# Modulation products of a two-layer diffusion step in groups of two blocks, their rows through GpSimd's queue

## The chip, the cores and the metric

One Trainium2 chip, one core. The metric is the device time of one execution in microseconds, as the median of three runs. The engines are TensorE (PE in the profile, its weight loads PEld), VectorE (DVE), ScalarE (ACT), GpSimd (POOL) and SyncE (SP), which only issues DMAs here. Each runs its own program in order and waits on semaphores of the others; DMAs issued from one engine stand in that engine's program too.

## The reference

Two layers over 128 context tokens and 512 latent tokens (640 columns), model width 1024. Every layer has six modulation vectors of 1024, for two conditioning vectors (context and latent):

```python
def _adaln(cond, w, b):
    return jax.nn.silu(cond) @ w + b

def _layer(x, mod, lw, lam_init, rope, ctx):
    sh1, sc1, g1, sh2, sc2, g2 = jnp.split(mod, 6, axis=-1)
    h = _rmsnorm(x, lw['norm1_g']) * (1.0 + sc1) + sh1
    mix, ctx_out = _mixers(h, lw, lam_init, rope, ctx)
    x = x + g1 * mix
    h = _rmsnorm(x, lw['norm2_g']) * (1.0 + sc2) + sh2
    x = x + g2 * _swiglu(h, lw['w_ffn_in'], lw['w_ffn_out'])
    return x, ctx_out
```

`_mixers` projects h to the inputs of retention, differential attention and latent attention (with compressed keys and values), merges the three branches by sigmoid gates and projects the result. The change concerns `silu(cond) @ w_ada`, a 1024 x 6144 matrix in each layer; in blocks of 128 columns that is 48 blocks a layer.

## The kernel before

Everything is float32, and the large matmuls are made of three products of rounded halves (names ending in hi and lo, `mm3`, line 134). A weight piece is loaded into one of three "raw" buffers by SyncE (`load_w`, line 126), ScalarE casts it to whi (line 118), VectorE forms wlo (line 121), and only then is the raw buffer free; whi and wlo have four buffers each.

The modulation is computed in three ways. In the beginning TensorE computes the first 16 blocks of layer 0. VectorE computes the blocks 16 to 39 of either layer in the retention's merge (`ada_rows`, its rows through GpSimd's queue into three "rawr" tiles). The others, blocks 40 to 47 of both layers and 0 to 15 of layer 1, are `ada_products`: 8 groups of four blocks. A group (l, j) loads four pieces of 512 KB, w_adap[l, j, i], by SyncE into the shared "raw" buffers (name rawp, line 265). Piece i holds the k-tiles 2i and 2i + 1, 512 columns each. The condition vector is stationary, 32 columns wide, two of them real; k-tile k goes to partition group k modulo 4 of one PSUM bank, G (line 269), so that four products can stand side by side in the array. ScalarE copies the bank to ada_r (line 272), four small matmuls with a selection matrix add up the partition groups and turn the result (line 276), VectorE adds the bias (line 279).

Where these groups stand is given by `plan` and `fill`: a list of steps from several generators, spread evenly over the fill points of a stage. In the latent attention (`mla`) the 30 steps of `diff_proj` (one projection of 128 tokens by 256 columns each, 24 matmuls, copied by ScalarE to stg, stored by GpSimd to the DRAM tile dproj, line 831) are mixed with 4 groups in layer 0 and 2 in layer 1, two steps a group. In the differential attention (`diff`) the gates (tile gt) and the values of the retention (tile gt, name rvs) are mixed with 2 groups in layer 0 and none in layer 1. While it fills, all of these take the same PSUM bank G. The tile framework then orders each engine's instructions by its own estimate of their times; it is the order that TensorE, SyncE and GpSimd follow.

Stages, in order, of each layer: mla, with w_mla, w_qp, w_qk, w_v as weights and normalised columns cqn turned and split (line 576, cqh, cql); the first branch (matmuls on yhi); diff, in which GpSimd loads V, rk, rq from dproj; retention (stores nret); merge with the other gates and branches, in which csr and rawr are loaded; output projection; FFN.

Of the kernel before, what the change touches and what calls it, by code (L numbers as in the profile page):

```python
# [12 lines left out]
F32 = mybir.dt.float32  # L13
# [8 lines left out]
P = 128  # L22
# [29 lines left out]
class Kern:  # L52
# [206 lines left out]
    def ada_products(self, pool, chunks):  # L259

        for l, j in chunks:
            ps = self.G()
            for i in range(4):
                raw = self.w.tile([P, 2, 512], F32, tag="raw", name="rawp", bufs=3)
                self.nc.sync.dma_start(out=raw, in_=self.io["w_adap"][l, j, i])
                for kk in range(2):
                    k = 2 * i + kk
                    g = k % 4
                    self.pe.matmul(ps[32 * g:32 * g + 32, :], self.cs[:, k, :], raw[:, kk, :],  # L269
                                   start=k < 4, stop=k >= 4, tile_position=(0, 32 * g))  # L270
            r = pool.tile([P, 512], F32, tag="ada_r", name="ada_r", bufs=1)
            self.act.copy(r, ps)
            yield 1
            ps = self.Tp()
            for c in range(4):
                self.pe.matmul(ps[:, 2 * c:2 * c + 2], r[:, 128 * c:128 * c + 128],
                               self.ct[:, C_SEL:C_SEL + 2], start=True, stop=True)
            b = self.pv[:, V_ADA + 48 * l + 4 * j:V_ADA + 48 * l + 4 * j + 4]
            self.dve.tensor_tensor(self.mod_tile(l)[:, 4 * j:4 * j + 4, :], ps[:, 0:8].rearrange("p (a v) -> p a v", v=2),
                                   b.unsqueeze(2).to_broadcast([P, 4, 2]), op=ALU.add)  # L280
            yield 1
# [1084 lines left out]
    def run(self):  # L1366
# [3 lines left out]
        for l in range(DEPTH):  # L1370
# [12 lines left out]
            with ExitStack() as c2:  # L1383
                pool = self.sb("mla", 1, c2)
                chunks = ((0, 10), (0, 11), (1, 0), (1, 1)) if l == 0 else ((1, 10), (1, 11))
                self.plan(37, (self.diff_proj(l, act, pool), 30, 0.0, 1.0), (self.ada_products(pool, chunks), 2 * len(chunks), 0.0, 1.0))
# [10 lines left out]
            chunks = ((1, 2), (1, 3)) if l == 0 else ()  # L1397
            self.plan(23, (self.gates(l, 2, act, m, mp), 16, 0.0, 0.7), (self.ret_values(l, act, mp), 20, 0.6, 0.95),
                      (self.ada_products(mp, chunks), 2 * len(chunks), 0.0, 0.7))
# [119 lines left out]
def layout(inputs):  # L1519
# [23 lines left out]
    out["w_adap"] = c(np.stack([[pieces(g["w_ada"][l][:, 512 * j:512 * j + 512], 2) for j in range(12)] for l in L]).reshape(DEPTH, 12, 4, 128, 2, 512))  # L1543
# [54 lines left out]
```

## Time and profile before

| | us |
|---|---|
| median of 3 runs | 2518.74 (2518.12 to 2518.92) |
| profiled execution | 2521.4 |
| its span, first to last instruction | 2519.6 |
| TensorE busy | 2415.9 (96%) |
| VectorE busy | 1769.7 (70%) |
| ScalarE busy | 1102.4 (44%) |
| GpSimd busy | 139.1 (6%) |
| mean granted clock of TensorE | 0.989 |

All later times come from the profiled execution. Busy is the time in which at least one instruction of the engine runs; matmuls overlap, so that a busy TensorE may still run at less than its full rate. The granted clock is a share of TensorE's upper level; 1.00 is 2.4 GHz, 0.50 is 1.2 GHz.

### The profile page before, as it was taken

To read this page: it belongs to the slowest core of one execution; us is meant where nothing else is said; L and a number is where in the kernel's file an instruction comes from. 1 tells how busy PE (TensorE), PEld (TensorE's weight loads), DVE (VectorE), ACT (ScalarE), POOL (GpSimd) and SP (SyncE) were. 2 spreads that over 40 slices of the span, in tenths; PEclk is the share of its full clock that TensorE was granted. 3 is DMA by queue.
4 is the path that set the end of the run, shared out by engine and by line. 5 is a ranking of instruction groups with operands and counts; after the bars stand their busy time and mean duration, and the time that the engine had idled before them with its cause. 6 is when DMAs were issued, how large, how long until landed. Compare 5 with 4: busy or idle time off the path is not lost.

```text
span 2519.6 us, 43242 instructions
## 1 busy us (share of the span) xinstructions
PE 2415.9 (96%) x16996; PEld 2330.6 (93%) x16996; DVE 1769.7 (70%) x3883; ACT 1102.4 (44%) x2265; POOL 139.1 (6%) x235
## 2 busy tenths in 40 slices
PE   8999999999999999999998999999999999999997
PEld 5899888999999999999987989989998999999997
DVE  5767677556688777767775766865666887777775
ACT  5555555522223633333374654655322354333334
POOL 0000211000010000000000002100000000000001
PEclk9999999999999999999999999999999999999999
DMA  6232423232454122222232122213215532222222
GB/s 265 78 102 86 133 99 104 79 114 68 151 176 133 53 92 75 89 77 73 78 123 83 60 94 88 89 55 110 84 65 197 166 93 74 86 76 82 76 73 72
DMA packets 81578, 250.02 MB, mean 99 GB/s; under 512 B 10624, under 2 KB 20064, under 8 KB 80352
## 3 DMA queue, kind: packets, MB, share of 16 engines
q1 hardware_dynamic: 58464, 180.91, 22.1%
q0 software_dynamic: 16864, 60.39, 7.3%
q10 hardware_dynamic: 6048, 5.98, 0.7%
q8 instruction: 133, 2.18, 0.4%
q14 instruction: 69, 0.57, 0.1%
HBM read 227.01 MB, written 20.22 MB: 98 GB/s over the span
## 4 chain that ended last, share of the span: by engine, by line
PE 81%; DVE 9%; ACT 3%; issue 3%; DMA 3%; POOL 0%; DVEq 0%; ACTq 0%; SPq 0%; POOLq 0%
PE G L134 33%; PE S L134 26%; PE Tp L134 7%; PE O L894 1%; PE S L1144 1%; PE S L1143 1%; PE S L1142 1%; PE Tp L697 1%; DVE wlo L121 1%; DVE x L1104 1%; ACT whi L118 1%; DMA rawp<-w_adap 1%; DVE v L1241 1%; PE G L269 1%; PE O L672 1%
## 5 line engine op out<-in xcount | busy, mean ns | idle before, releaser
L118 ACT CAST whi<-raw 128x1024 fp32r<-128x1024 f32 (+4 forms) x346 | 295.9, 858 | 463.8 <-PE S L134 174.2
L121 DVE TENSOR_TENSOR wlo<-raw,whi 128x1024 fp32r<-128x1024 f32 (+4 forms) x346 | 340.1, 985 | 138.6 <-ACT whi L118 136.8
L134 PE MATMUL G<-whi,hhi 128*128 128x256 f32 x1040 | 300.4, 289 | 8.0 <-DVE rvs L847 4.4
L134 PE MATMUL G<-whi,hlo 128*128 128x256 f32 x1040 | 295.9, 285 | 0.0
L134 PE MATMUL G<-wlo,hhi 128*128 128x256 f32 x1040 | 295.7, 284 | 0.0
L134 PE MATMUL G<-ghi,whi 128*128 128x320 f32 x704 | 220.5, 313 | 8.2 <-DVE x L1104 6.3
L134 PE MATMUL S<-hhi,whi 128*128 128x320 f32 x656 | 208.0, 317 | 10.1 <-DVE gt L1071 10.0
L134 PE MATMUL G<-ghi,wlo 128*128 128x320 f32 x704 | 217.4, 309 | 0.0
L134 PE MATMUL G<-glo,whi 128*128 128x320 f32 x704 | 217.4, 309 | 0.0
L134 PEld LDWEIGHTS G<-whi,hhi 128*128 128x128 f32 x1040 | 199.0, 191 | 12.9 <-DVE rvs L847 5.3
L134 PE MATMUL S<-hhi,wlo 128*128 128x320 f32 x656 | 205.0, 313 | 0.0
L134 PE MATMUL S<-hlo,whi 128*128 128x320 f32 x656 | 205.0, 313 | 0.0
L134 PEld LDWEIGHTS G<-wlo,hhi 128*128 128x128 f32 x1040 | 199.3, 192 | 0.1
L134 PEld LDWEIGHTS G<-whi,hlo 128*128 128x128 f32 x1040 | 199.1, 192 | 0.0
L134 PE MATMUL G<-hhi,whi 128*128 128x320 f32 x512 | 161.4, 316 | 8.3 <-DVE x L1104 4.1
L1104 DVE SCALAR_TENSOR_TENSOR x<-G,mod,x 128x128 f32<-128x128 f32 (+2 forms) x336 | 137.1, 436 | 41.9 <-PE G L134 40.7
L134 PE MATMUL G<-hhi,wlo 128*128 128x320 f32 x512 | 159.0, 311 | 0.0
L134 PE MATMUL G<-hlo,whi 128*128 128x320 f32 x512 | 158.5, 310 | 0.0
L134 PEld LDWEIGHTS G<-ghi,whi 128*128 128x128 f32 x704 | 132.1, 188 | 16.3 <-PE G L134 14.0
L487 DVE TENSOR_REDUCE mx<-S 128x1 f32<-128x640 f32 (+1 forms) x160 | 113.0, 714 | 43.3 <-PE S L865 24.8
L134 PEld LDWEIGHTS S<-hhi,whi 128*128 128x128 f32 x656 | 125.4, 191 | 13.7 <-DVE gt L1071 13.5
L134 PEld LDWEIGHTS G<-glo,whi 128*128 128x128 f32 x704 | 132.2, 188 | 0.2
(444 smaller groups left out, 6654.5 us busy)
## 6 DMA issues: line engine op xcount, KB each, us to landing
raw<-w_ffn_in SPq DMA_DIRECT2D x88, 512.0 KB, 3.7
raw<-w_gate SPq DMA_DIRECT2D x48, 512.0 KB, 3.4
rawr<-w_adat POOLq DMA_DIRECT2D x48, 512.0 KB, 4.0
rawp<-w_adap SPq DMA_DIRECT2D x32, 512.0 KB, 3.8
raw<-w_ffn_out SPq DMA_DIRECT2D x64, 256.0 KB, 2.7
raw<-w_diff SPq DMA_DIRECT2D x24, 512.0 KB, 3.9
raw<-w_branch SPq DMA_DIRECT2D x24, 512.0 KB, 3.7
raw<-w_ret SPq DMA_DIRECT2D x24, 512.0 KB, 3.5
```

The costliest lines, as they stand in the source:

```text
L118: (eng or self.act).copy(hi, src)
L121: (eng or self.dve).tensor_tensor(lo, src, hi.bitcast(F32), op=ALU.subtract)
L134: ins = self.pe.matmul(*args, **kw)
L269: self.pe.matmul(ps[32 * g:32 * g + 32, :], self.cs[:, k, :], raw[:, kk, :], start=k < 4, stop=k >= 4, tile_position=(0, 32 * g))
L487: self.dve.tensor_reduce(mx, sv, axis=AX.XY if len(sv.shape) == 3 else AX.X, op=ALU.max)
L672: self.pe.matmul(o[:, :n], vv, lo, start=False, stop=i == m - 1)
L697: self.pe.transpose(t[:, 256 * kb + 128 * i:256 * kb + 128 * i + 128], ps[i][:, 128 * (k0 + kb):128 * (k0 + kb) + 128], self.ident)
L894: pe.matmul(o[:, :128], at[:, 128 * kb:128 * kb + 128], V[:, kb0 + kb, :], start=kb == 0, stop=kb == nk - 1)
L1104: self.dve.scalar_tensor_tensor(x[h][:, n, c0:c1], ps[:, c0:c1], g[:, n, gi:gi + 1], x[h][:, n, c0:c1], op0=ALU.mult, op1=ALU.add)
L1142: self.pe.matmul(o, lh, rh, start=k == 0, stop=False)
L1143: self.pe.matmul(o, lh, rl, start=False, stop=False)
L1144: self.pe.matmul(o, ll, rh, start=False, stop=k == nk - 1)
```

## The change

`ada_products` works on groups of two blocks, 16 groups instead of 8. A group loads two pieces of 512 KB by GpSimd's queue into two tiles of its own ("rawp", in the pool of the stage); piece i holds the k-tiles 4i to 4i + 3, 256 columns each, so one piece feeds all four partition groups. The copy ada_r takes 256 columns and no tile of its own: in mla it is a third user of the two stg tiles, in diff of the two gt tiles. Two small matmuls instead of four follow. The list of steps has 16 instead of 8 ada steps in mla of layer 0, 8 instead of 4 in layer 1, and 8 instead of 4 in diff of layer 0. The bytes and the multiplications are the same.

```diff
--- before.py
+++ after.py
@@ -256,28 +256,26 @@
                 d.tensor_tensor(mod[:, b0:b1], mod[:, b0:b1], b.unsqueeze(2).to_broadcast([P, b1 - b0, 2]), op=ALU.add)
             yield 1
 
-    def ada_products(self, pool, chunks):
+    def ada_products(self, pool, rtag, chunks):
 
         for l, j in chunks:
             ps = self.G()
-            for i in range(4):
-                raw = self.w.tile([P, 2, 512], F32, tag="raw", name="rawp", bufs=3)
-                self.nc.sync.dma_start(out=raw, in_=self.io["w_adap"][l, j, i])
-                for kk in range(2):
-                    k = 2 * i + kk
-                    g = k % 4
-                    self.pe.matmul(ps[32 * g:32 * g + 32, :], self.cs[:, k, :], raw[:, kk, :],
-                                   start=k < 4, stop=k >= 4, tile_position=(0, 32 * g))
-            r = pool.tile([P, 512], F32, tag="ada_r", name="ada_r", bufs=1)
-            self.act.copy(r, ps)
+            for i in range(2):
+                raw = pool.tile([P, 4, 256], F32, tag="rawp", name="rawp", bufs=2)
+                self.pool.dma_start(out=raw, in_=self.io["w_adap"][l, j, i])
+                for g in range(4):
+                    self.pe.matmul(ps[32 * g:32 * g + 32, :256], self.cs[:, 4 * i + g, :], raw[:, g, :],
+                                   start=i == 0, stop=i == 1, tile_position=(0, 32 * g))
+            r = pool.tile([P, rtag[1]], F32, tag=rtag[0], name="ada_r", bufs=2)
+            self.act.copy(r[:, :256], ps[:, :256])
             yield 1
             ps = self.Tp()
-            for c in range(4):
+            for c in range(2):
                 self.pe.matmul(ps[:, 2 * c:2 * c + 2], r[:, 128 * c:128 * c + 128],
                                self.ct[:, C_SEL:C_SEL + 2], start=True, stop=True)
-            b = self.pv[:, V_ADA + 48 * l + 4 * j:V_ADA + 48 * l + 4 * j + 4]
-            self.dve.tensor_tensor(self.mod_tile(l)[:, 4 * j:4 * j + 4, :], ps[:, 0:8].rearrange("p (a v) -> p a v", v=2),
-                                   b.unsqueeze(2).to_broadcast([P, 4, 2]), op=ALU.add)
+            b = self.pv[:, V_ADA + 48 * l + 2 * j:V_ADA + 48 * l + 2 * j + 2]
+            self.dve.tensor_tensor(self.mod_tile(l)[:, 2 * j:2 * j + 2, :], ps[:, 0:4].rearrange("p (a v) -> p a v", v=2),
+                                   b.unsqueeze(2).to_broadcast([P, 2, 2]), op=ALU.add)
             yield 1
 
     def mod_scale(self, l, which):
@@ -1382,8 +1380,8 @@
             yraw = yp.tile([P, 4, T], F32, name="yraw")
             with ExitStack() as c2:
                 pool = self.sb("mla", 1, c2)
-                chunks = ((0, 10), (0, 11), (1, 0), (1, 1)) if l == 0 else ((1, 10), (1, 11))
-                self.plan(37, (self.diff_proj(l, act, pool), 30, 0.0, 1.0), (self.ada_products(pool, chunks), 2 * len(chunks), 0.0, 1.0))
+                chunks = [(0, j) for j in range(20, 24)] + [(1, j) for j in range(4)] if l == 0 else [(1, j) for j in range(20, 24)]
+                self.plan(37, (self.diff_proj(l, act, pool), 30, 0.0, 1.0), (self.ada_products(pool, ("stg", 256), chunks), 2 * len(chunks), 0.0, 1.0))
                 self.mla(l, act, yraw, pool, first)
                 self.flush()
             mctx = ExitStack()
@@ -1394,9 +1392,9 @@
             self.y_split(yhi, ylo, yraw, [(k, 0, T) for k in range(3)] + [(3, o, o + n) for o, n in HALF])
             yctx.close()
             self.branch_first(l, 2, yhi, ylo, m)
-            chunks = ((1, 2), (1, 3)) if l == 0 else ()
+            chunks = [(1, j) for j in range(4, 8)] if l == 0 else []
             self.plan(23, (self.gates(l, 2, act, m, mp), 16, 0.0, 0.7), (self.ret_values(l, act, mp), 20, 0.6, 0.95),
-                      (self.ada_products(mp, chunks), 2 * len(chunks), 0.0, 0.7))
+                      (self.ada_products(mp, ("gt", HW), chunks), 2 * len(chunks), 0.0, 0.7))
             with ExitStack() as c2:
                 self.diff(l, act, yhi, ylo, c2)
                 self.flush()
@@ -1540,7 +1538,7 @@
     wa = g["w_ada"][0]
     wa = np.concatenate([wa[:, :2048].reshape(D, 2, 4, 256).transpose(0, 2, 1, 3).reshape(D, 2048), wa[:, 2048:]], axis=1)
     out["w_ada"] = c(np.stack([pieces(wa[:, 512 * j:512 * j + 512], 2) for j in range(4)]).reshape(1, 4, 4, 128, 2, 512))
-    out["w_adap"] = c(np.stack([[pieces(g["w_ada"][l][:, 512 * j:512 * j + 512], 2) for j in range(12)] for l in L]).reshape(DEPTH, 12, 4, 128, 2, 512))
+    out["w_adap"] = c(np.stack([[pieces(g["w_ada"][l][:, 256 * j:256 * j + 256], 4) for j in range(24)] for l in L]).reshape(DEPTH, 24, 2, 128, 4, 256))
     out["w_adat"] = c(g["w_ada"].transpose(0, 2, 1).reshape(DEPTH, 48, 128, 1024))
     out["condr"] = c(np.broadcast_to(np.stack([g["c_ctx"], g["c"][0]])[None], (128, 2, 1024)))
     wi = g["w_in"]
```

What it does to the order. On SyncE, in the mla stage of layer 1, before (w_mla, w_diff and so on are the weights named above):

```order
L126 DMA raw<-w_mla 128x1024 x2
L126 DMA raw<-w_diff 128x1024 x2
L126 DMA raw<-w_qp 128x768
L265 DMA rawp<-w_adap 128x1024 x4
L126 DMA raw<-w_qk 128x640
L126 DMA raw<-w_v 128x512
L126 DMA raw<-w_diff 128x1024 x2
```

And after, at the same place of SyncE's program:

```order
L126 DMA raw<-w_mla 128x1024 x2
L126 DMA raw<-w_diff 128x1024 x2
L126 DMA raw<-w_qp 128x768
L126 DMA raw<-w_qk 128x640
L126 DMA raw<-w_v 128x512
L126 DMA raw<-w_diff 128x1024 x2
```

The four rawp transfers are gone from between w_qp and w_qk; the rest stands as it did, here and at the seven other places.

On GpSimd, in the mla stage of layer 0, before: all stores of the projection in a row.

```order
L527 DMA nkpe<-kp 128x32
L163 DMA avs<-cckv 128x256
L163 DMA avs<-rows 128x256
L550 DMA nckv<-ckvo 128x256
L831 DMA dproj<-stg 128x256 x30
L163 DMA ra<-rows 128x256
```

After (line numbers are lower by two from here on):

```order
L265 DMA rawp<-w_adap 128x1024 x2
L525 DMA nkpe<-kp 128x32
L163 DMA avs<-cckv 128x256
L163 DMA avs<-rows 128x256
L548 DMA nckv<-ckvo 128x256
L829 DMA dproj<-stg 128x256
L265 DMA rawp<-w_adap 128x1024 x2
L829 DMA dproj<-stg 128x256 x4
L265 DMA rawp<-w_adap 128x1024 x2
L829 DMA dproj<-stg 128x256 x3
```

The first pair of rawp stands ahead of the stage's other transfers, each later one between stores of dproj.

On TensorE, the first group of layer 1, before (ckh, ckl and cqh, cql are the split latents, hhi and hlo the normalised input):

```order
L134 MATMUL G<-whi,hhi 128x256
L134 MATMUL G<-wlo,hhi 128x256
L134 MATMUL G<-whi,hlo 128x256
L269 MATMUL G<-rawp,cs 32x512 x8
L134 MATMUL S<-ckh,whi 128x384
L134 MATMUL S<-ckl,whi 128x384
L134 MATMUL S<-cqh,whi 128x384
L134 MATMUL S<-cql,whi 128x384
```

And after:

```order
L552 MATMUL Tp<-ct,ckvn 128x128 x2
L574 MATMUL Tp<-ct,cqn 128x128 x3
L267 MATMUL G<-rawp,cs 32x256 x8
L134 MATMUL S<-ckh,whi 128x384
L134 MATMUL S<-ckl,whi 128x384
L134 MATMUL S<-ckh,wlo 128x384
L134 MATMUL S<-ckh,whi 128x384
L134 MATMUL G<-whi,cqh 128x256
```

The eight products now stand among the turns of cqn (line 574 here, 576 before), some hundred matmuls earlier; before, they came behind those and behind two more steps of the projection, ahead of the first matmul with w_qk (S<-ckh,whi).

## Rows read from the trace of the kernel before

**Rows 1.** The page: busy time of an engine; the last chain by engine.

```profile
PE 2415.9 (96%) x16996; PEld 2330.6 (93%) x16996; DVE 1769.7 (70%) x3883; ACT 1102.4 (44%) x2265; POOL 139.1 (6%) x235
...
PE 81%; DVE 9%; ACT 3%; issue 3%; DMA 3%; POOL 0%; DVEq 0%; ACTq 0%; SPq 0%; POOLq 0%
```

**Rows 2.** By stretch: length, busy us of each engine (instructions), clock, DMA share, GB/s.

```profile
63.22:302.33 239.11, 230.89 (x1770) 215.90 (x1768) 167.71 (x415) 135.94 (x332) 23.78 (x42) 0.99 0.29 98
302.33:540.65 238.32, 224.99 (x1706) 214.74 (x1707) 152.04 (x422) 123.78 (x321) 25.30 (x39) 1.00 0.33 104
540.65:653.65 113.00, 112.65 (x850) 110.77 (x849) 77.62 (x250) 29.08 (x48) 0.58 (x2) 1.00 0.19 64
1295.73:1547.01 251.28, 233.75 (x1748) 221.33 (x1746) 167.78 (x414) 137.22 (x332) 23.96 (x42) 0.97 0.25 81
1547.01:1775.24 228.23, 219.11 (x1658) 213.89 (x1659) 152.61 (x419) 121.45 (x318) 25.22 (x39) 0.99 0.28 90
```

**Rows 3.** TensorE in time, 400 us: start, length, operation, idle before and its releaser.

```profile
400.41 1.91 PE L269 MATMUL G<-rawp,cs 128*32 128x512 f32 x12 [0.53 <-ACT gt L1052]
402.25 0.77 PE L908 MATMUL Tp<-ct,osb 128*128 128x128 f32 x5
405.24 1.05 PE L269 MATMUL G<-rawp,cs 128*32 128x512 f32 x4 [2.23 <-DMA rawp<-w_adap]
406.23 1.05 PE L276 MATMUL Tp<-ct,ada_r 128*128 128x2 f32 x8
```

**Rows 4.** TensorE's waits (us in total, times, longest); rawp's landing.

```profile
PE G L269 <- DMA rawp<-w_adap: 9.6, 7, 3.1
...
DMA to landing us min/median/max: 3.4/3.8/5.3
```

**Rows 5.** SyncE in time, layer 1's mla stage, same columns.

```profile
1298.82 43.10 SPq L265 DMA_DIRECT2D rawp<-w_adap  x4
1342.01 0.39 SPq L126 DMA_DIRECT2D raw<-w_qk  x1
1342.49 0.38 SPq L126 DMA_DIRECT2D raw<-w_v  x1
1346.59 2.43 SPq L126 DMA_DIRECT2D raw<-w_diff  x2
```

**Rows 6.** TensorE in time, the same stage.

```profile
1345.50 1.05 PE L269 MATMUL G<-rawp,cs 128*32 128x512 f32 x4 [3.09 <-DMA rawp<-w_adap]
1347.86 0.69 PE L134 MATMUL S<-ckh,whi 128*128 128x384 f32 x1 [1.31 <-ACT whi L118]
...
1362.82 0.55 PE L134 MATMUL S<-kt,qt 96*128 96x128 f32 x3 [1.97 <-ACT pp L489]
```

**Rows 7.** GpSimd in time, the same stage: stores of the projection.

```profile
1340.74 0.54 POOL L831 DMA_DIRECT2D dproj<-stg  x1 [3.09 <-ACT stg L830]
1371.23 0.54 POOL L831 DMA_DIRECT2D dproj<-stg  x1 [29.95 <-ACT stg L830]
1376.69 0.54 POOL L831 DMA_DIRECT2D dproj<-stg  x1 [4.92 <-ACT avs L674]
```

**Rows 8.** By stretch, as rows 2: parts of the mla stages.

```profile
63.22:151.13 87.91, 83.24 (x625) 78.49 (x624) 62.06 (x180) 49.78 (x136) 6.59 (x12) 0.96 0.23 74
...
1295.73:1396.51 100.78, 90.41 (x640) 83.89 (x638) 62.62 (x178) 51.56 (x137) 6.67 (x13) 0.95 0.24 77
1396.51:1547.01 150.50, 143.34 (x1112) 137.43 (x1109) 105.16 (x237) 85.67 (x196) 17.30 (x30) 0.99 0.26 83
```

**Rows 9.** TensorE's waits on bank G around the groups, as rows 4.

```profile
PE G L269 <- ACT stg L830: 0.8, 2, 0.5
...
PE G L134 <- ACT ada_r L272: 0.6, 2, 0.3
```

**Rows 10.** The tile rawr: its DMA issues on GpSimd (ns, least/median/most) and landing.

```profile
L249 POOL DMA_DIRECT2D rawr<-w_adat x48: 531/531/537, 654.2 to 2024.0; - x48
...
DMA to landing us min/median/max: 3.6/4.0/8.7
```

## The prediction

> **What bounds the kernel now.** I read the page first. TensorE is busy 96% of the span and the chain that ended last runs through it for 81%; VectorE is at 70%, ScalarE at 44%, GpSimd at 6% [rows 1]. So work put on GpSimd has room, and time is won only where TensorE idles, runs at a lower clock, or does the same work in fewer steps.
>
> Next I cut the span by stages, at events that both layers have: the store of nkpe, the first branch matmul (on yhi), the store of nret. From the first to the second lies the latent attention (mla), from there to the third the differential attention (diff). The reader is to compare the layers [rows 2]. The matmuls of a stage are the same in both, except the modulation products: the mla stage of layer 0 holds four groups of four blocks and takes 239.11 us; that of layer 1 holds two and takes 251.28. The diff stage holds two groups in layer 0 (238.32) and none in layer 1 (228.23). What follows in layer 0, up to the load of csr, has no products, is 112.65 of 113.00 us busy, and its order is unchanged, so what the earlier stages gain should arrive at the end.
>
> What does a group cost on TensorE? In the group at 400 us [rows 3] the first twelve records last until the next operation starts: 402.25 - 400.41 = 1.84. The last four take 406.23 - 405.24 = 0.99, after an idle 2.23 that the DMA of rawp ended. The four transposes last 1.05. So a group is 1.84 + 0.99 + 1.05 = 3.9 us of work. With that, layer 1's mla stage is not 12.2 but 12.2 + 2 x 3.9 = **20 us** worse than layer 0's for the same rest.
>
> Why: the waits by tile and SyncE's queue. TensorE waits 9.6 us in seven places for rawp to land, a landing taking 3.8 [rows 4]. In layer 1 the four rawp transfers sit in SyncE's queue from 1298.82 to 1341.9; w_qk, w_v and the next w_diff, behind them in order, are issued only then [rows 5]. The three "raw" buffers are held by rawp pieces whose products stand far down TensorE's program; the fourth piece can't start until the first products have run. TensorE therefore waits 3.09 for it and 1.31 for the cast of w_qk [rows 6], and the projection that fills gaps has no weights: its stores pause from 1340.74 to 1371.23 [rows 7]. After idling, TensorE is granted less: a mean of 0.95 in the first part of that stage and 0.96 in layer 0's, that is stretches at the lower of its levels, 1.2 instead of 2.4 GHz; elsewhere it is 0.99 to 1.00 [rows 2, 8].
>
> **The change part by part.** The sum is made on the profiled run (2521.4 us, span 2519.6); the median of the plain runs, 2518.74, is 2.7 lower. Since the sum is a difference, I subtract it from the median.
>
> *Products in groups of two blocks.* Columns and multiplications are the same: 16 groups of 256 columns for 8 of 512. Before, piece 1 and 2 fed partition groups 0 to 3 side by side, and pieces 3 and 4 fed two groups each, piece 4 late: two rounds in 1.84 (0.92 each) and a third of 0.99. Now each piece holds all four groups, so a chunk is two rounds of half the columns: 0.92, and two chunks 1.84 plus some 0.07 for the second start. Saved: 8 x (2.83 - 1.91) = 7.4. Were a short round no cheaper than a long one, the saving would be 0. I take **-6**, near the row on which four groups run together. The transposes keep their number.
>
> *rawp leaves SyncE's queue and the "raw" buffers.* In layer 1's mla stage I set this against the 20 us. Its idle time is 251.28 - 233.75 = 17.5, layer 0's 239.11 - 230.89 = 8.2, so 9.3 more [rows 2]; the clock takes 0.05 x 100.78 + 0.01 x 150.50 = 6.5 against 0.04 x 87.91 = 3.5, so 3.0 more [rows 8]; the remaining 8 or so I can't place (matmuls without a neighbour to overlap). Ends: 9 and 20. I take **-15**, since idle and clock make 12.3 and part of the rest must go with them. Layer 0's mla stage has the same block earlier and milder: bounds 0 and 8 (its idle), and of those I take **-4.5**, mostly the clock's 3.5. Diff stage of layer 0: 238.32 - 228.23 = 10.1 for two groups whose work is 2 x 3.9 = 7.8; **-2.3**, ends 0 and 5.
>
> *Eight more groups through one PSUM bank.* While filling, every product and every projection uses the one bank G, and the next must wait for ScalarE's copy. Waits of this sort are there now: 0.5 and 0.3 us at most, in two of eight groups each [rows 9]. Eight more groups cost between 8 x (0.8 + 0.6) / 8 = 1.4 and 8 x (0.5 + 0.3) = 6.4; I take **+3**. The eight extra copies on ScalarE and adds on VectorE lie beside TensorE on engines with idle time: nothing, and if that cover is gone it is the wait just counted.
>
> *32 DMAs in GpSimd's queue.* The nearest row is rawr, the same 512 KB through the same queue: 0.531 us to issue [rows 10], 32 x 0.53 = 17 us on an engine idle 94% of the time. GpSimd works in order: a pair of rawp waits until the last chunk's products freed its two tiles, and behind it stand stores of dproj, and in the diff stage loads of V, rk and rq. By the order of the changed program a pair stands right behind the products that free it, and a chunk comes every 239 / 8 = 30 us in layer 0, so the pair has some 25 us to land. Cost 0; what it is if that fails is a rival. ada_r now takes one of two stg (or gt) tiles until its transposes; the other serves the projection, whose stores come some 5 us apart (1371.23, 1376.69) and need 0.54 to issue [rows 7]. Cost 0 to 1, in the +3.
>
> In this queue landing took 3.6 / 4.0 / 8.7 us (least, median, most), against 3.4 / 3.8 / 5.3 in SyncE's [rows 4, 10]. The Trainium skill (SBUF — State Buffer, section "SBUF: two separate sides", the trap "DVE blocks DMA") says that a DMA of GpSimd's queue has its descriptors written by GpSimd's own cores, and that VectorE locks these out while it runs a two-port fast mode, so that the transfer is late however idle the DMA engines are. By that rule this change moves 32 transfers into the worse queue; the median of rows 10 shows nearly nothing of it, the worst landing may.
>
> Sum: -6 - 15 - 4.5 - 2.3 + 3 = -24.8. 2518.74 - 24.8 = **2494**. All good ends give -7.4 - 20 - 8 - 5 + 1.4 = -39 (2480); all bad ends 0 - 9 - 0 - 0 + 6.4 = -2.6 (2516).
>
> **The rivals.** *Only the direct wait goes.* In the normalisation at the stage's start (cqn) TensorE waits also for VectorE and ScalarE, and the four whi/wlo buffers may hold weights back as the queue did. Then 9.6 of waits and 6 of rounds go, 3 come: -12.6, **2506**. For it: layer 1 also waits 1.97 for a softmax (pp) there [rows 6]. Against: layer 0 runs the same chain 20 us better.
>
> *Slower: GpSimd's queue blocks.* If a pair of rawp reaches the head of the queue before the products have run, the stores behind it stand, the one stg tile left isn't freed, the copy out of G waits, and TensorE with it. Place: the pairs among the dproj stores of both mla stages, twelve chunks. If each loses 4 us, 48 - 25 = +23: **2542**. It decides from 25 / 12 = 2.1 us a pair. Against: the order, and stores 5 us apart.
>
> *Slower: late landings.* If every chunk waited for the worst landing, 16 x (8.7 - 4.0) = 75, and 75 - 25 = +50: **2569**. That needs the lead of 25 us to be gone. The rule of the page named above would do this.
>
> *No effect.* Weights stay as late as now because something else holds them, and the handoffs eat the rounds: the bad ends, **2516**.
>
> *More than forecast*: all good ends, **2480**.
>
> **How the numbers follow.** Forecast 0.50 (2486 to 2502); direct wait only 0.20 (2502 to 2511); more 0.10 (2478 to 2486); no effect 0.09; slower 0.11 (blocking 0.08, landings 0.03). About 0.2% (5 us) is what a measurement of this kernel can tell from no change. Faster by more: 0.50 + 0.20 + 0.10 = 0.80 and a little of "no effect": 0.81. Within: 0.09. Slower: 0.10. The range 2478 to 2511 holds the first three cases, 0.80.
>
> **What would show it.** Right: no TensorE wait for rawp; w_qk of layer 1 issued within 10 us of w_qp; no pause of 30 us among the dproj stores; the mla stage of layer 1 shorter than layer 0's, near 232, with a clock of 0.98 or more; a chunk of products in about 0.95 us; the diff stage of layer 0 near 233. Wrong: the clock of the first part stays at 0.95, waits for cql, pp or whi grow in the place of rawp's, GpSimd idles before rawp while stores stand behind it, or a short round takes as long as a long one.

## The result and the profile after

The changed kernel takes 2492.9 us (median of four runs, 2491.6 to 2496.0), the kernel before 2518.6: the ratio is 0.9900, interval 0.9883 to 0.9917, that is 25.7 us less. 2494.0 was forecast, 24.8 less.

The total agrees; its parts have to be looked at one by one. The profiled run of after took 2491.57 us (span 2489.8), that of before 2521.4 (2519.6), so these two differ by 29.8. First the page of after: busy time of each engine, and the last chain by engine.

```profile
PE 2403.7 (97%) x17124; PEld 2328.7 (94%) x17124; DVE 1768.2 (71%) x3891; ACT 1104.0 (44%) x2273; POOL 155.9 (6%) x267
...
PE 86%; DVE 7%; ACT 3%; issue 2%; DMA 1%; DVEq 0%; ACTq 0%; POOLq 0%
```

Against [rows 1] the chain is more TensorE (86% for 81%) and the DMA's share fell from 3 to 1%. Then the stages of after, cut at the same events as [rows 2]: length, busy us of each engine, clock, DMA share, GB/s.

```profile
63.14:295.49 232.35, 227.47 (x1833) 216.15 (x1831) 166.64 (x419) 137.41 (x335) 29.45 (x54) 0.99 0.30 101
295.49:541.98 246.49, 230.04 (x1738) 222.21 (x1739) 152.34 (x424) 123.97 (x323) 31.46 (x51) 0.97 0.30 97
...
1292.41:1521.86 229.45, 224.84 (x1780) 216.07 (x1778) 167.89 (x416) 137.11 (x334) 27.04 (x48) 1.00 0.25 83
1521.86:1749.87 228.01, 218.82 (x1658) 213.70 (x1659) 151.91 (x419) 121.44 (x318) 25.15 (x40) 0.99 0.29 90
```

The mla stage of layer 0 is 6.8 us shorter (239.11 to 232.35), that of layer 1 21.8 (251.28 to 229.45); the diff stage of layer 0 is **8.2 longer** (238.32 to 246.49), at a clock of 0.97 where it was 1.00: TensorE idles 3.1 more there and is busy 5.1 longer. Together the three are 20.4 less. The rest stands where the change edits nothing: from the store of nret to the second load of x. The same view, that stretch of both layers, first before, then after:

```profile
540.65:678.47 137.82, 134.30 (x979) 132.16 (x978) 90.81 (x271) 38.31 (x65) 3.25 (x7) 0.98 0.27 93
1775.24:1913.90 138.66, 134.52 (x979) 132.38 (x978) 90.77 (x271) 38.34 (x65) 3.26 (x7) 0.98 0.26 91
```

```profile
541.98:674.53 132.55, 131.76 (x979) 129.62 (x978) 90.89 (x271) 38.33 (x65) 3.23 (x6) 1.00 0.28 94
1749.87:1883.67 133.80, 131.79 (x979) 129.65 (x978) 90.78 (x271) 38.34 (x65) 3.22 (x6) 1.00 0.27 95
```

5.3 and 4.9 us, with the same instructions. So -6.8 + 8.2 - 5.3 - 21.8 - 0.2 - 4.9 = -30.8, and all that is left of the program adds 1.0.

What was to be seen in the weights: SyncE in time in layer 1's mla stage (columns as [rows 5]), and what GpSimd waited for before an issue of rawp (us, times), and how long its landings took.

```profile
1290.65 0.33 SPq L126 DMA_DIRECT2D raw<-w_qp  x1
1295.49 0.33 SPq L126 DMA_DIRECT2D raw<-w_qk  x1
```

```profile
  PE G L267: 16.1, 10
  PE Tp L888: 15.4, 1
...
DMA to landing us min/median/max: 3.9/4.9/9.4
```

w_qk is issued 3.1 us after the stage begins, where it was 46.3 [rows 2, 5]. No wait of TensorE for rawp is left (9.6 us in [rows 4]). The landing became slower, and TensorE does not wait for it. The waits in the second fence are GpSimd's own: 16.1 us in ten places until products freed a tile, and 15.4 in one place, before the pair at 362.82 in the diff stage; GpSimd's next instruction behind that pair, at 376.53, waited 12.6 us more for ScalarE, so this wait held nothing that can be seen.

### The profile page after: what moved, and what is told of

It is laid out like the page before. It is cut to its first block, busy times and chain, and to the rows that moved or that the text cites. A ratio compares the mean times of both kernels' runs of the same rounds, so it can differ in the third digit from the quotient of the medians.

```text
span 2489.8 us, 43494 instructions
## 1 busy us (share of the span) xinstructions
PE 2403.7 (97%) x17124; PEld 2328.7 (94%) x17124; DVE 1768.2 (71%) x3891; ACT 1104.0 (44%) x2273; POOL 155.9 (6%) x267
## 3 DMA queue, kind: packets, MB, share of 16 engines
q1 hardware_dynamic: 53856, 164.13, 20.4%
## 4 chain that ended last, share of the span: by engine, by line
PE 86%; DVE 7%; ACT 3%; issue 2%; DMA 1%; DVEq 0%; ACTq 0%; POOLq 0%
PE G L134 36%; PE S L134 26%; PE Tp L134 7%; PE O L892 2%; PE S L1142 1%; PE Tp L695 1%; PE S L1141 1%; PE S L1140 1%; DVE wlo L121 1%; DVE x L1102 1%; PE Tp L888 1%; PE O L670 1%; PE O L669 1%; PE S L862 1%; PE S L863 1%
## 5 line engine op out<-in xcount | busy, mean ns | idle before, releaser
L134 PEld LDWEIGHTS G<-ghi,wlo 128*128 128x128 f32 x704 | 132.2, 188 | 0.0
```

The source lines that it names most:

```text
L134: ins = self.pe.matmul(*args, **kw)
```

## The experiments

**The whole as one table.** All lengths come from the profiled run of each kernel; "w_qk" is how long after the start of layer 1's mla stage its first issue stands; "between" runs from layer 0's nret to layer 1's nkpe. The cuts are rounded to 0.1 us, so that a last digit can be off by one. Each ratio is to runs of the kernel before on the same chip; its medians there lie between 2516.2 and 2518.6, so that differences of medians from different chips carry 1 to 2 us of that. The names of the runs are explained below.

| kernel | us (ratio to before) | mla 0 | diff 0 | between | w_qk | mla 1 |
|---|---|---|---|---|---|---|
| before | 2518.6 | 239.1 | 238.3 | 755.1 | 46.3 | 251.3 |
| b_pool | 2521.7 (1.0011, 0.9999 to 1.0023) | 245.5 | 239.0 | 758.2 | 45.1 | 245.7 |
| b_raw4 | 2499.0 (0.9926, 0.9914 to 0.9937) | 238.9 | 233.8 | 750.6 | 46.2 | 243.7 |
| g_pool_raw | 2516.5 (0.9998, 0.9983 to 1.0012) | 241.5 | 249.7 | 755.9 | 18.3 | 233.7 |
| g_sp_raw | 2512.4 (0.9971, 0.9955 to 0.9987) | 238.9 | 253.6 | 755.2 | 18.7 | 234.7 |
| g_raw4 | 2491.5 (0.9903, 0.9888 to 0.9917) | 234.1 | 244.3 | 750.6 | 8.4 | 229.7 |
| g_sp_own | 2494.7 (0.9910, 0.9889 to 0.9931) | 232.5 | 247.0 | 750.6 | 3.1 | 229.3 |
| after | 2492.9 (0.9900, 0.9883 to 0.9917) | 232.4 | 246.5 | 750.4 | 3.1 | 229.5 |
| two_four | 2480.6 (0.9867, 0.9851 to 0.9884) | 232.3 | 233.1 | 750.1 | 3.1 | 229.2 |

A stage is read from one execution, and executions of one program differ. The run b_csr_pool (below) edits the kernel before only behind the load of csr; up to there in layer 0 TensorE, VectorE and ScalarE execute the same instructions in the same order, and its mla stage of layer 0 takes 239.5, its diff stage 241.6 where before has 239.1 and 238.3. Its diff stage, columns as [rows 2]:

```profile
303.10:544.70 241.60, 230.50 (x1705) 219.78 (x1706) 152.05 (x422) 123.97 (x321) 25.23 (x39) 0.97 0.33 105
```

So some three us of one stage are not yet a difference between kernels. The profiled execution can also lie off its median: that of g_sp_raw took 2517.2 (its twelve runs 2503.4 to 2517.6), that of b_pool 2525.6.

**Grouping alone (g_sp_raw).** The theory on trial: SyncE's queue stood still behind rawp pieces whose products are far down TensorE's program.

```diff
-                raw = pool.tile([P, 4, 256], F32, tag="rawp", name="rawp", bufs=2)
-                self.pool.dma_start(out=raw, in_=self.io["w_adap"][l, j, i])
+                raw = self.w.tile([P, 4, 256], F32, tag="raw", name="rawp", bufs=3)
+                self.nc.sync.dma_start(out=raw, in_=self.io["w_adap"][l, j, i])
```

> The grouping alone: groups of two blocks, but rawp goes through SyncE's queue into the three shared raw buffers, as before the change. Theory (what cost was SyncE's queue standing still behind rawp pieces whose products are far down TensorE's program; a long standstill needs four pieces for three buffers): two pieces fit in the three buffers, so SyncE is held less, but it still stands before the next pair. The rounds' 6.6 us come, handoffs cost some 3, and about half of the 22 + 7 us of the two mla stages: 2505 (2500 to 2512), with layer 1's mla stage near 240. Rival A (the number of pieces per group was all that cost): as the changed kernel, 2493, layer 1's mla stage near 230. Rival B (buffers shared with the weights cost as much with two pieces): 2515, layer 1's mla stage near 250.

**Own tiles, SyncE's queue (g_sp_own):** only the second of these lines is changed.

> Groups of two blocks and two tiles of their own for rawp, but filled from SyncE's queue. Theory (a pair of rawp waits at the head of an in-order queue until the last chunk's products are done, and weights stand behind it): in SyncE's queue that holds w_qk and w_diff back, so the time is 2500 to 2510 and layer 1's mla stage 235 to 245; TensorE waits for casts of weights come back. Rival A (the tiles are what matters, the queue not, since each pair stands right behind the products that free it): 2493, within 3 us of the changed kernel.

**Shared buffers, GpSimd's queue (g_pool_raw):** only the first.

> Groups of two blocks through GpSimd's queue, but into the three shared raw buffers. Theory (a piece of rawp that waits for its products holds a raw buffer, and weights need three for casts of two halves): SyncE's weights have one or two buffers left while a pair waits, SyncE is held by the buffers and not by the queue; 2498 to 2506, layer 1's mla stage 233 to 242. Rival A (only the queue matters): 2493. Rival B (only the buffers matter): as with SyncE's queue and shared buffers, within 3 us of that run.

**The kernel before with rawp through GpSimd's queue (b_pool):** one line.

```diff
-                self.nc.sync.dma_start(out=raw, in_=self.io["w_adap"][l, j, i])
+                self.pool.dma_start(out=raw, in_=self.io["w_adap"][l, j, i])
```

> The kernel before with rawp through GpSimd's queue, all else unchanged: groups of four blocks, four pieces into the three shared raw buffers. Theory (SyncE's weights must not stand behind a piece that waits for its products): w_qk no longer stands behind the fourth piece in order, but finds its buffers held; 2508 to 2516, the wait of TensorE for rawp stays near 9, and the dproj stores stand behind the fourth piece in GpSimd's queue, which may make it slower than before, 2525. Rival (the queue is all): 2500, the weights of layer 1's mla stage issued as early as in the changed kernel.

The queue is worth no time. With own tiles SyncE's queue gives 2494.7, GpSimd's 2492.9; the stages agree to 0.5 us. With shared buffers GpSimd's queue is by its median 4 us slower than SyncE's, and in the kernel before it changes nothing that can be told in the total, while its two mla stages move by +6 and -6 us. The column of w_qk shows why: 18.3 and 18.7, 45.1 and 46.3. Whichever queue rawp takes, w_qk comes at the same time, since it waits for a buffer, not for its turn. In g_pool_raw GpSimd stands instead. Its waits before an issue of rawp:

```profile
  DVE wlo L121: 101.7, 7
  DVE z L488: 26.8, 2
  PE G L267: 19.7, 9
```

101.7 us until a weight's second half (wlo) was made, that is until a shared buffer came free, with the stores of dproj behind. The theory of a blocked queue, as the expectations of the first two runs put it, fell; rival A of g_sp_own stands. Three of these four forecasts missed their ranges. g_sp_raw (2500 to 2512 expected) took 2512.4: its mla stage of layer 1 came down by 16.6 us, and its diff stage of layer 0 grew by 15.2. g_pool_raw (2498 to 2506) took 2516.5, near its rival B, and b_pool (2508 to 2516) 2521.7.

**Buffers (b_raw4, g_raw4).** The kernel before, and the grouping alone, with four shared buffers.

```diff
-        raw = self.w.tile([P, cols], F32, tag="raw", name="raw", bufs=3)
+        raw = self.w.tile([P, cols], F32, tag="raw", name="raw", bufs=4)
```

> The kernel before with four shared raw buffers instead of three, all else unchanged: groups of four blocks in SyncE's queue. Theory (the fourth piece needs a buffer that the first holds until its products have run, and w_qk stands behind it): with four buffers the four pieces are issued at once, but w_qk behind them still needs a buffer; the wait for rawp (9.6 us on TensorE) goes, the weights stay late: 2506 to 2513. Rival A (the fourth piece alone is what blocks): 2498 to 2502, since only rounds (6.6) are missing. Rival B (SyncE's order matters, not the number of buffers): 2517.

> Groups of two blocks through SyncE's queue with four shared raw buffers in place of three, no tiles of their own: one 4 KB buffer less than with two own tiles. What ran so far: three shared buffers 2512.4 (mla stages 238.9 and 234.7, diff stage of layer 0 253.6), two own tiles 2494.7 (232.5, 229.3, 247.0). Theory (what counts is how many buffers the weights still have while a pair of rawp waits: one with three, two with four, three with own tiles; a pair of weights needs two): most of the gain comes with the fourth, 2496 to 2501, mla stages near 233 and 231. Rival (tiles must be apart, since a weight behind a rawp piece in the same ring of buffers waits for its products whatever the ring's length): 2505 to 2512, mla stages near 238 and 234.

One number in the kernel before gives 18.3 us, seven tenths of what the whole change gives, and more than the theory's range of 2506 to 2513 held; g_raw4 too lies below its theory's 2496 to 2501. The 2499.0 of b_raw4 is the time of its rival A, but its mla stage of layer 1 is still 243.7 with w_qk at 46.2, so the weights stayed late as the theory said. Of the 24.1 us between the two profiled executions 7.8 lie in the mla stages, 4.6 in the diff stage of layer 0, and 10.5 in the two stretches from nret to the second load of x, which come under the pause at csr below. With groups of two, the fourth buffer is worth 20.9 by the medians (2512.4 to 2491.5) and 17 by the two ratios, the two own tiles 17.7 and 15. Layer 1's mla stage, by stretch (columns as [rows 2]), in b_raw4, g_sp_raw and g_raw4:

```profile
1286.50:1530.20 243.70, 228.71 (x1749) 217.27 (x1748) 167.55 (x414) 137.26 (x332) 23.82 (x42) 0.99 0.26 84
```

```profile
1310.50:1545.20 234.70, 226.80 (x1780) 217.80 (x1779) 167.27 (x416) 136.98 (x334) 23.67 (x42) 0.99 0.27 87
```

```profile
1293.20:1522.90 229.70, 225.02 (x1781) 216.02 (x1779) 168.52 (x416) 137.44 (x334) 23.84 (x42) 1.00 0.26 87
```

Count the buffers that are left for weights while one group of rawp is in them: before none, for four pieces want three; b_raw4 none; g_sp_raw one; g_raw4 two; own tiles three. The stage takes 251.3, 243.7, 234.7, 229.7, 229.3. It falls until a pair of weights finds room, and no further. So for this stage grouping, tiles and a fourth buffer are ways to the same thing, and the queue is none. TensorE's direct wait for rawp is a part only: b_raw4 has none left, is 7.6 us better than before with as few buffers left, and still 14 behind g_raw4.

**Why the diff stage of layer 0 grew.** Three causes were tried. A tile of its own for ada_r, in place of a gt tile (own_r):

```diff
-            r = pool.tile([P, rtag[1]], F32, tag=rtag[0], name="ada_r", bufs=2)
+            r = pool.tile([P, 256], F32, tag="ada_r", name="ada_r", bufs=1)
```

> The changed kernel with a tile of its own for ada_r (256 columns, one buffer) in place of one of the two stg or gt tiles. The diff stage of layer 0 became 8.2 us longer with the change, where 2.3 shorter was forecast; TensorE idles twice there for 2.3 and 2.8 us with no gate matmuls between transposes. Theory (ada_r takes one of the two gt tiles, so that gate units move away from the places where TensorE needs them): 4 to 8 us faster than the changed kernel, 2485 to 2489, the diff stage of layer 0 near 239 with a clock of 0.98 or more. Rival (the tile does not matter, it is the number of steps or their place): within 2 us of 2493, the diff stage unchanged near 246.

It fell: 2500.5 us (0.9931, 0.9910 to 0.9952; the interval overlaps that of after), by the medians 7.6 more than after, and the stage is longer still:

```profile
295.20:546.50 251.30, 231.26 (x1738) 222.64 (x1739) 151.57 (x424) 124.08 (x323) 31.48 (x51) 0.96 0.29 95
```

The four groups moved to the mla stage (mla12):

```diff
-                chunks = [(0, j) for j in range(20, 24)] + [(1, j) for j in range(4)] if l == 0 else [(1, j) for j in range(20, 24)]
+                chunks = [(0, j) for j in range(20, 24)] + [(1, j) for j in range(8)] if l == 0 else [(1, j) for j in range(20, 24)]
-            chunks = [(1, j) for j in range(4, 8)] if l == 0 else []
+            chunks = []
```

> The changed kernel with all twelve groups of layer 0 in its mla stage and none in its diff stage. Theory: from the first branch matmul to the second load of x layer 0 takes 379.0 us with four groups in the diff stage, layer 1 takes 361.8 for the same work without; four groups cost 17 there, and in the mla stage 4 x 2 = 8 us of work. So 9 less: 2484 (2480 to 2488), that stretch of layer 0 near 363, its mla stage near 241. Rival (the mla stage can't take them: pairs of rawp come too close, a chunk each 19 us, and GpSimd's queue stands before them): the mla stage grows by 15 or more, 2492 or slower.

2498.0 us (0.9927, 0.9914 to 0.9941); its mla and diff stage of layer 0:

```profile
63.60:317.10 253.50, 238.85 (x1913) 223.20 (x1911) 168.20 (x424) 138.09 (x339) 36.27 (x64) 0.98 0.32 107
317.10:543.80 226.70, 217.53 (x1658) 212.23 (x1659) 152.23 (x419) 122.79 (x319) 25.27 (x40) 1.00 0.29 90
```

The diff stage gives back 19.8, and the mla stage takes 21.1 where 8 was the theory's price; its idle time goes from 4.9 to 14.7 (length less TensorE's busy time). The rival stands in its size, though GpSimd isn't the place: its wait before rawp is 13.1 us here and 16.1 in after. Four more groups of two cost 20 in either stage, for some 6 us of work (1.00 for the products of each, below, and half of the 1.05 of [rows 3] for its transposes).

Two groups of four in the diff stage, once with four shared buffers (h4), once with the mla stages of after (two_four). The new step, for both:

```diff
+            ps = self.G()
+            for h in range(2):
+                for i in range(2):
+                    ...
+                    for g in range(4):
+                        self.pe.matmul(ps[32 * g:32 * g + 32, 256 * h:256 * h + 256], self.cs[:, 4 * i + g, :], raw[:, g, :],
+                                       start=i == 0, stop=i == 1, tile_position=(0, 32 * g))
+            r = pool.tile([P, 512], F32, tag="ada_r", name="ada_r", bufs=1)
+            self.act.copy(r, ps)
```

> As the run with groups of two, SyncE's queue and four shared raw buffers, but in the diff stage of layer 0 two groups of four blocks (512 columns, one copy of 512, four transposes in one step) in place of four groups of two; same pieces, same rounds of 256 columns. Theory (in the diff stage each group costs a pass through bank G, a copy and a step between softmax units, so four groups cost about 20 there and two about 7 to 12): the diff stage of layer 0 takes 232 to 238 in place of 247 to 254, and the kernel is 10 to 15 us faster than the one without this edit. Rival (the rounds of 256 columns or the shared buffers make the diff stage longer, not the number of groups): within 4 us of it, the diff stage 245 or more.

> The changed kernel in its mla stages (groups of two, two own tiles, GpSimd's queue), but in the diff stage of layer 0 two groups of four blocks, as the edit of the run before this one: one own tile and the three shared raw buffers take the four pieces, through SyncE's queue. Theory (the diff stage lost by the number of groups): mla stages as in the changed kernel, 232.4 and 229.5, the diff stage of layer 0 near 234 (the kernel before with four raw buffers had 233.8 with two groups of four), so 12 less than the changed kernel: 2481 (2478 to 2485), which beats both. Rival (the growth has another cause): diff stage 244 or more, 2490 to 2496.

h4 takes 2484.7 us (0.9876, 0.9860 to 0.9892; four runs from 2480.9 to 2489.3), 6.8 less than g_raw4 where 10 to 15 were expected, with 239.4 in the stage where 232 to 238 were; two_four 2480.6, as its theory said, and it beats both kernels (its four runs, 2479.5 to 2487.1, lie below those of after). The stage in h4, then in two_four:

```profile
298.30:537.70 239.40, 228.01 (x1737) 221.51 (x1738) 151.65 (x422) 124.47 (x321) 25.28 (x39) 0.97 0.33 105
```

```profile
295.30:528.40 233.10, 224.66 (x1737) 217.25 (x1738) 151.92 (x422) 123.71 (x321) 28.30 (x44) 0.99 0.33 105
```

Two groups for four are worth 13.4 against after, 4.9 against g_raw4. Over all profiled executions this stage took 233.1 to 241.6 with two groups of four (before, b_pool, b_raw4, h4, two_four and the two csr runs), 244.3 to 253.6 with four groups of two (six kernels, with either queue, with shared or own tiles, with or without a tile for ada_r), and 226.7 with none. What the steps displace is seen on TensorE in time, in after (idle before and its releaser in brackets), and by stretch around it:

```profile
397.35 0.77 PE L888 MATMUL Tp<-ct,dp 128*128 128x128 f32 x5 [2.31 <-DVE ylo L121]
...
434.27 0.75 PE L804 MATMUL Tp<-identr,qs 128*128 128x128 f32 x4 [2.83 <-DVE mx L486]
```

```profile
400.00:410.00 10.00, 10.00 (x57) 10.00 (x56) 3.39 (x11) 4.06 (x15) 0.00 (x0) 0.68 0.01 2
...
430.00:440.00 10.00, 5.69 (x31) 4.95 (x31) 7.53 (x26) 4.23 (x10) 0.00 (x0) 0.68 0.16 52
440.00:450.00 10.00, 9.88 (x70) 9.68 (x69) 3.65 (x12) 4.58 (x17) 1.07 (x2) 0.81 0.14 40
```

At 397 and 434 no gate matmuls stand between the transposes, TensorE idles 2 to 3 us on VectorE, and stretches behind are granted 0.68 and 0.81 in the mean, that is in part the lower of the two levels, 1.2 of 2.4 GHz. In two_four the largest idle of the stage is 1.30. That the stage's length goes with the number of groups is shown by the two ranges, which do not overlap. That it works by the missing gate matmuls is argued from after alone: the tile scheduler lays these instructions in another order in each kernel, and no run holds that order still. The clock is in part the execution's: h4 has 0.97 here in the profiled run, and b_csr_pool 0.97 with the order for which before has 1.00.

**The pause at csr (b_csr_pool, two_four_csr).** Where the two stretches from nret to the second load of x differ, TensorE idles once in each layer of before. In after the idle at this place is 0.43 us in layer 0 and 1.65 in layer 1. Before, then layer 1 of after:

```profile
665.05 0.64 PE L134 MATMUL S<-hhi,whi 128*128 128x320 f32 x1 [3.17 <-DVE gt L1071]
...
1900.26 0.63 PE L134 MATMUL S<-hhi,whi 128*128 128x320 f32 x1 [3.79 <-DVE gt L1071]
```

```profile
1872.77 0.42 PE L134 MATMUL S<-hhi,whi 128*128 128x320 f32 x1 [1.65 <-DVE gt L1069]
```

VectorE's gate (gt) stands behind its first pass over csr (csth), and that waits for csr's load. VectorE in time, layer 0, in before and in after:

```profile
662.24 2.36 DVE L235 SCALAR_TENSOR_TENSOR csth<-csth,csr 128x1024 f32<-128x1024 f32 x2 [8.17 <-ACT csth L234]
664.51 0.48 DVE L1071 SCALAR_TENSOR_TENSOR gt<-gt,S 128x320 f32<-128x320 f32 x1
```

```profile
659.37 2.36 DVE L235 SCALAR_TENSOR_TENSOR csth<-csth,csr 128x1024 f32<-128x1024 f32 x2 [3.99 <-ACT csth L234]
```

And csr's load in GpSimd's queue, with its landing in the two layers, before and after:

```profile
653.65 0.55 POOL L163 DMA_DIRECT2D csr<-condr  x1 [112.42 <-DVE gt L1071]
...
1888.23 0.55 POOL L163 DMA_DIRECT2D csr<-condr  x1 [112.41 <-DVE gt L1071]
...
DMA to landing us min/median/max: 7.5/7.7/8.0
```

```profile
643.53 0.55 POOL L163 DMA_DIRECT2D csr<-condr  x1 [100.98 <-PE O L1001]
...
1862.88 0.55 POOL L163 DMA_DIRECT2D csr<-condr  x1 [112.43 <-DVE gt L1069]
...
DMA to landing us min/median/max: 5.1/5.5/5.9
```

In layer 0 it is issued 113.0 us after nret before and 101.6 after; in layer 1 113.0 in both, but it lands in 5.9 us where it took 8.0. The other runs show that the landing sets the pause. Leaving out the two runs that follow, 18 loads are issued 113.0 to 113.4 us after nret; they land in 5.5 to 8.3 us, and TensorE's pause is in each 4.2 to 4.4 less than the landing. The six loads issued earlier (101.5 to 102.1, once 110) leave no idle above 0.44.

Does the shorter pause belong to the change? In layer 0 three of the four others with own tiles have it too: g_sp_own, own_r and two_four take 132.6 for the stretch, mla12 136.0. In layer 1 three of the four do not: in g_sp_own, own_r and two_four csr lands in 8.3, 7.7 and 7.5 us, and the stretch takes 138.7, 137.1 and 136.9; mla12 has 5.7 and 133.6. Up to there TensorE runs g_sp_own in the order of after, but for one transposition in layer 0. Layer 1 of g_sp_own, the stretch and the pause:

```profile
1750.42:1889.15 138.73, 134.27 (x979) 132.13 (x978) 90.72 (x271) 38.31 (x65) 3.22 (x6) 0.98 0.27 91
```

```profile
1875.76 0.64 PE L134 MATMUL S<-hhi,whi 128*128 128x320 f32 x1 [4.11 <-DVE gt L1069]
```

So the 5.3 us of layer 0 mostly come back with own tiles, and that the change makes the 4.9 of layer 1 is not shown. To see whether VectorE's order is the whole of the pause, the passes were given to GpSimd, in the kernel before and in two_four:

```diff
-            d.scalar_tensor_tensor(th, th, 1.0, cs[:, i, :], op0=ALU.add, op1=ALU.mult)
-            d.tensor_scalar(cs[:, i, :], th, 0.5, None, op0=ALU.mult)
+            self.pool.tensor_scalar(th, th, 0.5, 0.5, op0=ALU.mult, op1=ALU.add)
+            self.pool.tensor_tensor(cs[:, i, :], th, cs[:, i, :], op=ALU.mult)
```

> The kernel before, but the two passes over csr behind the tanh (csth) run on GpSimd instead of VectorE: th/2 + 1/2 and a multiplication by csr, the same values by another form. Why: the stretch from the store of nret to layer 1's nkpe, outside all filled stages, is 755 us in the kernels with three shared raw buffers and 750.5 in those with four or with own tiles; in the former csr is loaded 113 us after nret, VectorE stands 8.2 us before csth, the gate of the branch (gt) behind it is late and TensorE idles 3.2 (layer 0) and 3.8 us (layer 1). Theory (VectorE held by csth is the whole of it): both idles go, 4 to 5 us a layer with the clock, 2517 becomes 2508 (2505 to 2511), the stretch 750.5. Rival (GpSimd's passes are slower and stand before the loads of rawr and x in its queue, so that the sums over rawr or the x load come late): 2515 or more.

> The fastest kernel so far (groups of two blocks in own tiles in the mla stages, two groups of four in the diff stage, 2480.55) with the same edit: the two passes over csr on GpSimd. There layer 0 has no idle at csth left, layer 1 still 3.3 us. Theory: 4 us less, 2476.5 (2474 to 2479). Rival (GpSimd's passes delay its queue): 2480 or more.

Neither is faster: the first takes 2524.1 us (1.0026, 1.0015 to 1.0038), the second 2484.5 (0.9878, 0.9862 to 0.9893), which can't be told from two_four. The times are the rivals', the reason is another one. In b_csr_pool TensorE's first gate matmul behind csr's load waits 0.51 us, so the pause of 3.17 is gone from there. A new one stands ten us further down:

```profile
676.54 0.41 PE L134 MATMUL S<-hhi,whi 128*128 128x320 f32 x1 [2.77 <-DVE gt L1071]
```

VectorE in time ahead of it, and GpSimd's multiplications by csr:

```profile
665.92 0.49 DVE L1071 SCALAR_TENSOR_TENSOR gt<-gt,S 128x320 f32<-128x320 f32 x1 [7.78 <-PE S L134]
666.44 1.33 DVE L1072 TENSOR_TENSOR m<-m,gt 128x320 f32<-128x320 f32 x1
667.70 3.42 DVE L121 TENSOR_TENSOR wlo<-raw,whi 128x1024 fp32r<-128x1024 f32 x1
671.04 3.91 DVE L121 TENSOR_TENSOR ylo<-yraw,yhi 128x320 fp32r<-128x320 f32 x4
```

```profile
667.41 5.99 POOL L236 TENSOR_TENSOR csr<-csth,csr 128x1024 f32<-128x1024 f32 x2
```

VectorE no longer waits for csr and works without a gap up to the next gate. But while GpSimd runs its passes, the same subtraction (wlo) that takes VectorE 1.22 us elsewhere takes 3.42, and four of the ylo, 0.49 each elsewhere, take 3.91. The gate comes late by that. So holding VectorE was the first pause, and the remedy makes another one of nearly the same size; two_four_csr shows 3.43 and 3.91 in layer 1; in its layer 0 GpSimd has ended before the four ylo, and they take 1.69. Why csr is issued earlier in layer 0 of after, and why its landing varies, stays open. With four shared raw buffers it landed in 5.2 to 5.7 us (six loads), with three shared in 6.4 to 8.1 (ten), with own tiles in 5.1 to 8.3 (twelve), and no run moved only that.

## Why the prediction was right, and where not

*Products: -6; measured -6.6.* The row of a chunk, in TensorE's time of after: a chunk from 81.11 to the next start at 82.11, 1.00 us, for 2.83 / 2 a half group before, so 8 x (2.83 - 2.00) = 6.6. The forecast's 0.92 is reached where two chunks stand in a row: two_four runs 32 matmuls from 391.55 to 393.41, 0.93 a chunk.

```profile
81.11 1.07 PE L267 MATMUL G<-rawp,cs 128*32 128x256 f32 x16
82.11 0.44 PE L552 MATMUL Tp<-ct,ckvn 128*128 128x128 f32 x2
```

```profile
391.55 1.93 PE L290 MATMUL G<-rawp,cs 128*32 128x256 f32 x32 [0.53 <-ACT gt L1073]
393.41 0.76 PE L929 MATMUL Tp<-ct,osb 128*128 128x128 f32 x5
```

*Layer 1's mla stage: -15, with its products and handoffs -15.8; measured -21.8.* The prediction gave two reasons in one: the weights stand behind rawp in SyncE's order, and rawp holds the three raw buffers. The second is what b_raw4 and g_raw4 show; b_pool, g_pool_raw and g_sp_own show that the order cost nothing. What went wrong is the size. The step took layer 0's stage as the floor: idle 9.3 more, clock 3.0 more. But layer 0 had the same fault, and its own idle fell too. Against the true floor, layer 1's idle went from 17.5 to 4.6 (-12.9) and its busy time from 233.75 to 224.84 (-8.9): by an estimate from the two rounded means 0.03 x 251.3 = 7.5 of that is the clock, from 0.97 to 1.00, and the products of 4 of the 16 groups, 4 / 16 of 6.6, are the rest. Idle and clock thus account for the 8 us that the prediction couldn't place.

*Layer 0's mla stage: -4.5, with products and handoffs -6.0; measured -6.8.* This term was right.

*Diff stage of layer 0: -2.3, with products and handoffs -3.1; measured +8.2.* The wrong sign. The step set 10.1 us for two groups against 7.8 us of work and wanted the difference back. It counted the groups' work, and for their doubled number it had only the handoff, 0.75 of the +3: by mla12 a group of two costs 5 us there, for 1.5 of work. Of the 8.2 some three may be the profiled execution's clock, as b_csr_pool shows. The direct handoff through bank G was not sized too small: TensorE's waits for the copy of ada_r are 1.8 us in three places, 0.6 before [rows 9].

*What follows in layer 0: "its order is unchanged, so what the earlier stages gain should arrive"; measured -5.3, and -4.9 in layer 1.* [rows 2] cut that stretch at the load of csr, just ahead of the pause. Looking 12 us further would have shown TensorE's idle of 3.17. The gain of layer 0 comes back in three of the four other kernels with own tiles, that of layer 1 in one, and why the landing differs is open.

*GpSimd's queue: 0; measured 0.* g_sp_own against after, 2494.7 and 2492.9 with overlapping intervals. The landing rose from 3.8 to 4.9 us and at worst from 5.3 to 9.4, but the queue alone is less: with the tiles held (before and b_pool, g_sp_raw and g_pool_raw, g_sp_own and after) GpSimd's queue adds 0.4 to 0.5 to the median and 1.6 to 2.7 to the worst. That agrees in sign with the trap "DVE blocks DMA" of the Trainium skill (SBUF — State Buffer, "SBUF: two separate sides"); that VectorE is the cause, no run here shows. The rival of late landings needed the lead to be gone, and TensorE waits for no rawp. The rival of a blocked queue didn't come either: GpSimd does idle before rawp, 16.1 and 15.4 us, which was named as a sign of being wrong, but the longest pause among the dproj stores is 22.4 us, where before has 30.5. A standing queue is seen in g_pool_raw, 101.7 us, where the tiles are not rawp's own.

So the total is right partly by luck. Against the forecast the diff stage is 11.3 worse, layer 1's mla stage 6.0 better, layer 0's 0.8, and 10.2 came that no term held, 4.9 of it from a landing that three of four like kernels do not have; with the remaining +0.8 that is -4.9, and the two profiled runs lie 4.1 further apart (29.8) than the medians (25.7).

## What to carry to other kernels

When loads of two kinds share a ring of buffers, count the buffers that the one kind leaves to the other while it waits for its consumer: one buffer more, or pieces that fit, may be most of what a new queue and new tiles seem to bring. A fill that is cut into more steps can pay per step and not per multiplication (here 5 us for 1.5 of work), so try it whole as well as cut. Before a gain in one stage is credited to a change, look whether the same order of instructions shows it in a second execution. Where two stretches of a program are compared to find what a fault costs, ask whether the better one has the same fault in a milder form.

## What was not expected of the hardware

In the diff stage of before TensorE idles 2.23 us at 405 [rows 3] and 2.73 at 532, and the clock of the stage is 1.00 [rows 2]. In b_csr_pool, with the same order of instructions, it idles 2.07 and 2.73 in the same two places; the stretch from 405 to 415 is granted 0.51, the ten us behind the second idle 0.83, and the stage has 0.97. So the same idle is followed by the lower level in one execution and not in another. While GpSimd multiplied two tiles of 128x1024, a subtraction of that size on VectorE took 3.42 us for 1.22. The 512 KB of rawp land in 3.7 to 5.0 us (medians by kernel and queue); the worst were 6.7 from SyncE's queue and 9.8 from GpSimd's (two_four_csr), both with own tiles. The same load of csr took 5.1 to 8.3 us by kernel and layer, and with it a pause of TensorE came and went.
